# A two-layer decoder trunk on one core: expert tiles turned on another engine, gates placed a step later, scores a step later, one affine cut into pieces

## The chip, the cores and the metric

The kernel runs as one program on 1 core of one Trainium2 chip. The metric is the device time of that core in microseconds, the median of the runs shown. The core has five engines with in-order instruction queues of their own: TensorE (PE, with its weight loads shown as PEld), VectorE (DVE), ScalarE (ACT), GpSimd (POOL) and SyncE (SP, which here only issues DMAs).

## The reference

The computation is a decoder trunk with D = 1024, 256 tokens, batch 1 and 2 layers. Each layer does two things to the residual x:

```python
# part 1: two token mixers side by side
mod = silu(c) @ w_ada[l] + b_ada[l]                  # six rows: shift, scale, gate, twice
hm  = x * (1 + sc1) + sh1
qa, fa, ia, ga, qb, kb, vb, gate_a, gate_b = split(hm @ w_in[l])
oa  = rms_norm(hgrn2(qa, fa, ia)) * silu(ga)         # S_t = f_t S_{t-1} + (1-f_t) v_t, o_t = S_t' q_t
ob  = stick_breaking_attention(qb, kb, vb)
y   = (sigmoid(gate_a) * (oa @ w_up_a) + sigmoid(gate_b) * (ob @ w_up_b)) @ w_o
x   = layer_norm(ALPHA * x + y * gt1, ln_g[l, 0], ln_b[l, 0])
# part 2: product-key experts: 16384 experts of one neuron each, 8 heads, 16 chosen per head and token
hf  = x * (1 + sc2) + sh2
idx, gates = top16 of the sums of two top16 lists of 128 keys, softmax     # per token and head
y   = sum over the chosen experts of gate * gelu(hf . peer_u[idx]) * peer_v[idx]
x   = layer_norm(ALPHA * x + y * gt2, ln_g[l, 1], ln_b[l, 1])
```

## The kernel before

**Precision and matmuls.** Every float32 weight is split into a high part (`wh`, a rounded copy made by ACT) and a low part (`wl`, the rest, a subtraction made by POOL or DVE, line 271). A product is three matmuls: high by high, high by low, low by high (`products`, line 63). Nearly all of them go through `mm` at line 61, so the profile puts them on one line; what they write tells them apart: `A` is the expert scores, `Y` the expert output, `T`, `G` and `K` are further PSUM tiles.

**How weights arrive.** `order` (lines 101 to 177) is one list of all weight tiles of 128 x 1024 in the order of their use. `take` (line 302) hands the next one out: it first issues the DMA of a later tile (`fetch`, on SP's queue), then has the tile after the current one split (`prep`, line 227: ACT makes `wh`, POOL or DVE makes `wl`), and then has the next `u` tile turned (`turn`, line 215). All engines get their instructions in this written order; nothing is reordered later.

**The mixers** (`mixers`, line 656). The projections walk over weight tiles, 24 matmuls each. After each tile `project` calls `pull` (line 635), which lets a side generator issue some of its own work: first `decays`, then `hgrn`, then `stick`. `hgrn` (line 819) computes the intra-sequence scores of the recurrence as a tree of 9 levels (sizes 256, 128, ..., 2, 1). Level i goes through four stages: exponents (`st_exp`: two DVE subtractions, one ACT exponential), products (`st_mul`: two DVE multiplications into a tile named `qk`), scores (`st_score`: 8 or 4 small matmuls) and placing (`st_place`: two masked DVE copies). Step i of its loop (line 890) issues placing of level i-3, scores of level i-2, products of level i-1 and exponents of level i, and ends with `yield None`, which lets `pull` do no more than one step for each weight tile. `qk` has two buffers; `stick` and, at the start of the program, the loads of `w_ada` (`mtile`, line 1060) use the same tile name, and SP waits in order until a buffer is free.

**The experts** (`peer`, line 1319). Instead of gathering experts, all 16384 are computed densely. 128 `u` tiles give the scores (`u_tile`, line 1623: 24 matmuls of 128 x 128 by 128 x 256), 128 `v` tiles the output (line 1710 on: 12 matmuls of 512 columns). The gates are zero where an expert was not chosen. A `u` tile must be turned so that the model dimension lies on the partitions, and there are two ways for it. Kind "u" is loaded in rows of 1 KB and turned in 32 x 32 blocks by one DVE instruction (line 220). Kind "x" is loaded in pieces of 128 bytes, and is turned by 8 TensorE transposes (line 251), after which ACT copies each half out of PSUM twice (lines 263 and 264). `uv_seq` (line 124) makes every fourth tile an "x".

Beside the `u` tiles runs one side generator, `select`. First `topk` finds the 16 best of each head (many small DVE instructions, then for each half of the tokens the selection from line 1449, with six large DVE instructions of 128 x 2048). Then `place_gates` (line 1492) goes through 64 blocks of 4 tokens. For each block, `build` makes two one-hot tiles (DVE, lines 1499 and 1504), `prod` multiplies them into a PSUM tile `G` (8 small matmuls), and `put` writes the result to the activations: by ACT where the scores of an expert tile are not there yet, by a DVE multiplication (line 1531) where they are. Step b issues `prod` of block b-1, `build` of block b, then `put` of block b-1.

**The budget.** Each `u` tile calls `pull(sides, 1.55 + 1.2 * (kind == "x"))` (line 1642). Each `yield c` of a generator takes c from this credit, a negative credit ends the turn, and `yield None` ends it too. The numbers c are meant as microseconds of DVE, but they are only what is written there. After tile 125 whatever is left of the side work is issued at once (`drain`, line 1645).

**The affine of the first norm** is applied late: at `v` tiles 38 and 44 (line 1725), POOL multiplies one half of x by the row `g_row` and adds `b_row`, in whole instructions of 128 x 1024. Both rows come by a POOL-issued DMA (`load_row`) into space that `v` tiles 12 to 19 set free.

Of the kernel before, what the change touches and what calls it, by code (L numbers as in the profile page):

```python
# [16 lines left out]
P = 128  # L17
# [28 lines left out]
def trunk_kernel(ctx: ExitStack, tc: tile.TileContext, x, c, w_ada, b_ada, w_in, lb_logits, hg_norm_g,  # L46
# [76 lines left out]

    uv_seq = [("x" if j % 4 == 3 else "u", j) for j in range(NK)] + [("v", j) for j in range(NK)]
    for l in range(DEPTH):
# [530 lines left out]
    def mixers(l, hT):  # L656
        with ExitStack() as es:
# [161 lines left out]
            def hgrn():  # L819
# [28 lines left out]
                def st_mul(i):  # L848
                    n = sizes[i]
                    if n == 1:  # L850
                        return
                    hn = n // 2
                    t = ap.tile([P, HG_H, S], F32, name="qk", bufs=2)
                    ev = es_.pop(i)
                    tv = nodes(t, n)
                    nc.vector.tensor_mul(tv[:, :, :hn], nodes(kk, n)[:, :, :hn], ev[:, :, :hn])
                    nc.vector.tensor_mul(tv[:, :, hn:], nodes(qT, n)[:, :, hn:], ev[:, :, hn:])  # L857
                    qk[i] = t
# [30 lines left out]
                n = len(sizes)  # L889
                for i in range(n + 3):  # L890
                    if 0 <= i - 3 < n:
                        st_place(i - 3)
                    if 0 <= i - 2 < n:
                        st_score(i - 2)
                    if 0 <= i - 1 < n:
                        st_mul(i - 1)
                    yield 2.4
                    if i < n:
                        st_exp(i)
                    yield None  # L900
# [44 lines left out]
            def stick():  # L945
# [17 lines left out]
                def mask(z, a):  # L963
                    sp = ap.tile([P, HG_H, S], F32, name="qk", bufs=2).rearrange("p h t -> p (h t)")[:, :384]
                    nc.vector.scalar_tensor_tensor(sp, z[:, :384], 0.0, a, op0=OP.max, op1=OP.add)
# [79 lines left out]
            def start():  # L1045
# [14 lines left out]
                def mtile():  # L1060
                    names.rotate(1)
                    return ap.tile([P, HG_H, S], F32, name=names[0], bufs=2).rearrange("p h t -> p (h t)")

# [171 lines left out]
            else:  # L1235
# [16 lines left out]
                    (("f_z", 1), ("qT", 1), ("qbT", 1), ("kbT", 1), ("v_a", 1), ("v_b", 1), ("kk", 1), ("bb", 1),  # L1252
                     ("gaT", 1), ("sc0", 1), ("e", 2), ("e", 2), ("qk", 2), ("qk", 2))]
            free = deque(a[:, i] for a in free for i in range(2))
# [64 lines left out]
    def peer(l, hT):  # L1319
        with ExitStack() as es:  # L1320
# [11 lines left out]
            with ExitStack() as eu:  # L1332
# [26 lines left out]
                def topk():  # L1359
# [89 lines left out]
                    for tt in range(2):  # L1449

                        puf = pu[tt].rearrange("p h k -> p (h k)").bitcast(U32)
                        for a in range(2):
                            nc.vector.tensor_scalar(sel[a].bitcast(U32), puf, 4 - 2 * a, None,
                                                    op0=OP.logical_shift_right)
                            nc.vector.tensor_copy(half[2 + a], iu[a][tt].rearrange("p h k -> p (h k)").bitcast(U32))

                        nc.vector.scalar_tensor_tensor(half[0], sel[1].bitcast(U32), -12.0, sel[0].bitcast(U32),
                                                       op0=OP.add, op1=OP.max)
                        for a in range(2):
                            nc.vector.scalar_tensor_tensor(sel[a], half[0], -16.0 + 12 * a, puf, op0=OP.mult, op1=OP.add)  # L1460
                        nc.vector.scalar_tensor_tensor(half[1], sel[1], -48.0, sel[0], op0=OP.add, op1=OP.max)
                        tp = top[tt]
                        yield 0.9
                        for a in range(2):
                            nc.vector.tensor_tensor(m, per_head(half[a])[:, :, :, None].to_broadcast(k4),
                                                    iota_k[:, None, None].to_broadcast(k4), op=OP.is_equal)
                            yield 1.4
                            nc.vector.tensor_mul(m, m, per_head(half[2 + a])[:, :, None].to_broadcast(k4))
                            yield 1.1
                            nc.vector.tensor_reduce(per_head(sel[a]), m, axis=mybir.AxisListType.X, op=OP.add)  # L1470
                            yield 1.4
                        nc.vector.tensor_reduce(sm[:, :PH], tp, axis=mybir.AxisListType.X, op=OP.add)
# [19 lines left out]
                def place_gates():  # L1492
# [26 lines left out]
                    def put(b, pg):  # L1519
# [12 lines left out]
                        progress["t"] = (b + 1) * TB  # L1532

                    built, prods = {}, {}
                    nb = S // TB
                    for b in range(nb + 1):
                        if 0 <= b - 1 < nb:
                            prods[b - 1] = prod(b - 1)
                        if b < nb:
                            build(b)  # L1540
                        yield 1.2
                        if 0 <= b - 1 < nb:
                            put(b - 1, prods.pop(b - 1))

                        yield 0.2 + 0.7 * progress["j"] / NK
                        yield None
# [163 lines left out]
                for kind, j in uv_seq[nu:]:  # L1710
# [13 lines left out]

                    if j in (NB_J + 6, NB_J + 12):
                        xb = from_blocks(xt[j // 6 - (NB_J + 6) // 6])
                        nc.gpsimd.tensor_mul(xb, xb, in_blocks(g_row))
                        nc.gpsimd.tensor_add(xb, xb, in_blocks(b_row))
                    mod_step(mods_left)
# [55 lines left out]
```

## Time and profile before

| What | Value |
|---|---|
| median of 3 runs | 2251.29 us (2247.49 to 2252.64) |
| profiled execution | 2254.38 us, its span 2252.6 us, granted TensorE clock 0.982 |
| busy: PE, DVE, ACT, POOL | 2135.2, 1817.2, 1172.5, 1041.5 us |
| HBM read | 396.46 MB, 176 GB/s over the span |

The stages of layer 0 as the trace shows them: start to about 105 us, tree of scores to 160 us, other mixer work to 303 us, `u` tiles from about 309 to 777 us, `v` tiles to about 1135 us. Layer 1 repeats them from there (tree 1214 to 1262 us, `u` tiles to 1883 us, `v` tiles to 2230 us).

A row of the groups reads: line, engine, operation, what it writes and reads, shape, count, then busy time in us and the mean of one in ns, then idle time of the engine just before and what ended it. A row of a window reads: the stretch, its length, busy time (and count of instructions) of PE, PEld, DVE, ACT and POOL, then the granted clock, the DMA share and GB/s. A row of the timeline reads: start, length, engine, line, operation, count, and in brackets the idle time before it. A matmul's own duration is longer than the distance between two of them, since they overlap; so PE's costs are taken from busy time and from periods.

### The profile page before, as it was taken

To read this page: it belongs to the slowest core of one execution; us is meant where nothing else is said; L and a number is where in the kernel's file an instruction comes from. 1 tells how busy PE (TensorE), PEld (TensorE's weight loads), DVE (VectorE), ACT (ScalarE), POOL (GpSimd) and SP (SyncE) were. 2 spreads that over 40 slices of the span, in tenths; PEclk is the share of its full clock that TensorE was granted. 3 is DMA by queue.
4 is the path that set the end of the run, shared out by engine and by line. 5 is a ranking of instruction groups with operands and counts; after the bars stand their busy time and mean duration, and the time that the engine had idled before them with its cause. 6 is when DMAs were issued, how large, how long until landed. Compare 5 with 4: busy or idle time off the path is not lost.

```text
span 2252.6 us, 42211 instructions
## 1 busy us (share of the span) xinstructions
PE 2135.2 (95%) x14596; PEld 1945.4 (86%) x14596; DVE 1817.2 (81%) x3278; ACT 1172.5 (52%) x2445; POOL 1041.5 (46%) x760
## 2 busy tenths in 40 slices
PE   5789899899999999999989998998999999999998
PEld 5789799899999978888779897997999999788886
DVE  7887989999997488888887558999999955666675
ACT  3446555455555545555545564554555555455562
POOL 4656637787778510000045534577777783200001
PEclk8999999999999999999999999999999999999999
DMA  8646567666667678888844335675766676666662
GB/s 273 196 137 221 159 140 159 129 148 148 142 147 156 176 236 275 281 286 283 298 134 150 113 121 142 147 153 118 154 142 148 146 164 187 202 196 192 193 227 90
DMA packets 498895, 400.32 MB, mean 178 GB/s; under 512 B 291920, under 2 KB 446072, under 8 KB 498680
## 3 DMA queue, kind: packets, MB, share of 16 engines
q1 hardware_dynamic: 496936, 392.33, 62.8%
q0 software_dynamic: 1408, 4.23, 0.6%
q8 instruction: 115, 1.88, 0.3%
q10 hardware_dynamic: 336, 1.06, 0.1%
q14 instruction: 100, 0.82, 0.1%
HBM read 396.46 MB, written 1.05 MB: 176 GB/s over the span
## 4 chain that ended last, share of the span: by engine, by line
PE 73%; DVE 16%; DMA 4%; issue 3%; ACT 3%; POOL 1%; SPq 1%; POOLq 0%; ACTq 0%; DVEq 0%
PE A L61 28%; PE Y L61 27%; PE T L61 7%; PE G L61 4%; PE T L251 2%; DVE wl L271 2%; PE ss L61 2%; PE hs L61 2%; DMA raw<-in_peer_u_dram 2%; POOL wl L271 1%; DVE qk L857 1%; DMA raw<-in_peer_v_dram 1%; DVE raw L220 1%; DVE e L843 1%; DVE o L1504 1%
## 5 line engine op out<-in xcount | busy, mean ns | idle before, releaser
L271 POOL TENSOR_TENSOR wl<-raw,wh 128x512 fp32r<-128x512 f32 x663 | 914.3, 1406 | 700.9 <-ACT wh L58 582.4
L58 ACT ACTIVATE wh<-raw 128x512 fp32r<-128x512 f32 x1060 | 610.8, 623 | 182.0 <-PE A L61 47.6
L61 PE MATMUL A<-hTh,wh 128*128 128x256 f32 x2080 | 543.3, 293 | 11.9 <-ACT wh L58 11.8
L61 PE MATMUL A<-hTl,wh 128*128 128x256 f32 x2080 | 524.2, 284 | 0.0
L61 PE MATMUL Y<-wh,o 128*128 128x512 f32 x1776 | 480.5, 392 | 0.8 <-DVE o L521 0.8
L271 DVE TENSOR_TENSOR wl<-raw,wh 128x512 fp32r<-128x512 f32 x525 | 380.2, 765 | 63.5 <-ACT wh L58 44.9
L61 PEld LDWEIGHTS A<-hTh,wh 128*128 128x128 f32 x2080 | 400.6, 193 | 14.4 <-ACT wh L58 13.7
L61 PEld LDWEIGHTS A<-hTl,wh 128*128 128x128 f32 x2080 | 401.7, 193 | 0.8 <-DVE hTl L521 0.2
L61 PEld LDWEIGHTS Y<-wh,o 128*128 128x128 f32 x1776 | 334.9, 189 | 70.8 <-DVE o L521 1.2
L61 PE MATMUL A<-hTh,wl 128*128 128x256 f32 x2080 | 337.9, 285 | 11.0 <-POOL wl L271 10.9
L61 PEld LDWEIGHTS A<-hTh,wl 128*128 128x128 f32 x2080 | 288.9, 193 | 14.2 <-POOL wl L271 14.2
L61 PE MATMUL Y<-wl,o 128*128 128x512 f32 x888 | 277.9, 393 | 10.4 <-DVE wl L271 10.4
L220 DVE STREAM_TRANSPOSE raw<-raw 128x1024 f32<-128x1024 f32 x192 | 235.1, 1230 | 11.7 <-DMA raw<-in_peer_u_dram 10.1
L58 ACT ACTIVATE o<-buf 128x256 fp32r<-128x256 f32 x228 | 95.1, 417 | 282.7 <-PE Y L61 282.7
L521 DVE TENSOR_TENSOR o<-buf,o 128x256 fp32r<-128x256 f32 x228 | 100.1, 439 | 150.4 <-ACT o L58 150.4
L61 PEld LDWEIGHTS Y<-wl,o 128*128 128x128 f32 x888 | 168.1, 189 | 48.9 <-DVE wl L271 13.8
L1499 DVE TENSOR_TENSOR o<-iT,iota_t 128x1024 f16<-128x1024 f16 x128 | 163.9, 1280 | 0.0
L58 ACT ACTIVATE buf<-G 128x128 f32<-128x128 f32 (+4 forms) x244 | 56.0, 276 | 203.6 <-PE G L61 203.6
L570 POOL TENSOR_TENSOR x<-x,buf 128x1024 f32<-128x1024 f32 x1 | 2.4, 2392 | 291.0 <-DVE x L567 291.0
L61 PE MATMUL T<-hTh,wh 128*128 128x256 f32 x512 | 133.6, 293 | 0.0
L61 PE MATMUL T<-hTl,wh 128*128 128x256 f32 x512 | 130.1, 286 | 0.0
L1504 DVE TENSOR_TENSOR o<-gT,o 128x1024 f16<-128x1024 f16 x128 | 124.6, 973 | 4.4
(496 smaller groups left out, 3254.9 us busy)
## 6 DMA issues: line engine op xcount, KB each, us to landing
raw<-in_peer_u_dram SPq DMA_DIRECT2D x1024, 128.0 KB, 3.5
raw<-in_peer_v_dram SPq DMA_DIRECT2D x256, 512.0 KB, 4.4
raw<-in_w_in_dram SPq DMA_DIRECT2D x88, 512.0 KB, 4.9
raw<-in_w_ada_dram SPq DMA_DIRECT2D x78, 512.0 KB, 4.9
raw<-in_w_o_dram SPq DMA_DIRECT2D x16, 512.0 KB, 3.5
raw<-in_w_pq_dram SPq DMA_DIRECT2D x64, 128.0 KB, 3.4
qk<-in_w_ada_dram SPq DMA_DIRECT2D x10, 512.0 KB, 3.9
e<-in_w_ada_dram SPq DMA_DIRECT2D x8, 512.0 KB, 6.0
```

What stands on the lines that cost most here:

```text
L58: nc.scalar.activation(o, i, f, **kw)
L61: nc.tensor.matmul(o, a, b, start=start, stop=stop, **kw)
L220: nc.vector.transpose(t, t)
L251: nc.tensor.transpose(banks[s][:, q], t[:, (4 * s + q) * P:(4 * s + q + 1) * P], ident)
L271: eng.tensor_sub(lo, src, h.bitcast(F32))
L521: nc.vector.tensor_sub(lo, src, h.bitcast(F32))
L570: nc.gpsimd.tensor_mul(xt[tt], xt[tt], last[0])
L843: eng.tensor_sub(ev[:, :, :hn], mid, bv[:, :, :hn])
L857: nc.vector.tensor_mul(tv[:, :, hn:], nodes(qT, n)[:, :, hn:], ev[:, :, hn:])
L1499: nc.vector.tensor_tensor(o.rearrange("p a u n v -> p (a u) n v"), iT[:, b].rearrange("p a (u v) -> p (a u) v", v=2)[:, :, None] .to_broad ...
L1504: nc.vector.tensor_mul(og.rearrange("p u a n v -> p (u a) n v"), gT[:, b * nu:(b + 1) * nu].rearrange("p u a v -> p (u a) v")[:, :, None] ...
```

## The change

- **Tiles turned.** In the second half of the `u` tiles (j from 64 on) kind "x" becomes "u": 16 tiles in each layer lose their 8 TensorE transposes and two of four ACT copies, and get one DVE transpose and the loads in rows of 1 KB instead of 128 bytes. Their budget falls from 2.75 to 1.55.
- **Block order.** `place_gates` puts block b-2 first, then builds block b, then multiplies block b-1; so a `put` comes a step after its `prod`. There is one more step.
- **Budget of the selection.** More yields and larger numbers: 13.0 instead of 8.7 for each half of the tokens up to line 1471. The instructions stay the same.
- **Tree.** Scores of level i-3 and placing of level i-4 instead of i-2 and i-3, one more step, three `qk` buffers instead of two; with that the `w_ada` loads at the start get a third `qk` buffer too.
- **Affine in pieces.** 16 POOL instructions of 128 x 256 at `v` tiles 38 to 53, instead of 4 of 128 x 1024 at tiles 38 and 44.

```diff
-    uv_seq = [("x" if j % 4 == 3 else "u", j) for j in range(NK)] + [("v", j) for j in range(NK)]
+    uv_seq = [("x" if j % 4 == 3 and j < NK // 2 else "u", j) for j in range(NK)] + [("v", j) for j in range(NK)]
...
-                    t = ap.tile([P, HG_H, S], F32, name="qk", bufs=2)
+                    t = ap.tile([P, HG_H, S], F32, name="qk", bufs=3)
...
-                for i in range(n + 3):
+                for i in range(n + 4):
+                    if 0 <= i - 4 < n:
+                        st_place(i - 4)
                     if 0 <= i - 3 < n:
-                        st_place(i - 3)
-                    if 0 <= i - 2 < n:
-                        st_score(i - 2)
+                        st_score(i - 3)
                     if 0 <= i - 1 < n:
                         st_mul(i - 1)
                     yield 2.4
...
-                    return ap.tile([P, HG_H, S], F32, name=names[0], bufs=2).rearrange("p h t -> p (h t)")
+                    return ap.tile([P, HG_H, S], F32, name=names[0], bufs=3 if names[0] == "qk" else 2).rearrange("p h t -> p (h t)")
...
                         for a in range(2):
                             nc.vector.tensor_scalar(sel[a].bitcast(U32), puf, 4 - 2 * a, None,
                                                     op0=OP.logical_shift_right)
+                            yield 0.5
                             nc.vector.tensor_copy(half[2 + a], iu[a][tt].rearrange("p h k -> p (h k)").bitcast(U32))
+                            yield 0.6
 
                         nc.vector.scalar_tensor_tensor(half[0], sel[1].bitcast(U32), -12.0, sel[0].bitcast(U32),
                                                        op0=OP.add, op1=OP.max)
+                        yield 0.5
                         for a in range(2):
                             nc.vector.scalar_tensor_tensor(sel[a], half[0], -16.0 + 12 * a, puf, op0=OP.mult, op1=OP.add)
+                            yield 0.5
                         nc.vector.scalar_tensor_tensor(half[1], sel[1], -48.0, sel[0], op0=OP.add, op1=OP.max)
                         tp = top[tt]
-                        yield 0.9
+                        yield 0.5
                         for a in range(2):
                             nc.vector.tensor_tensor(m, per_head(half[a])[:, :, :, None].to_broadcast(k4),
                                                     iota_k[:, None, None].to_broadcast(k4), op=OP.is_equal)
-                            yield 1.4
+                            yield 1.7
                             nc.vector.tensor_mul(m, m, per_head(half[2 + a])[:, :, None].to_broadcast(k4))
                             yield 1.1
                             nc.vector.tensor_reduce(per_head(sel[a]), m, axis=mybir.AxisListType.X, op=OP.add)
-                            yield 1.4
+                            yield 1.6
...
-                    for b in range(nb + 1):
-                        if 0 <= b - 1 < nb:
-                            prods[b - 1] = prod(b - 1)
+                    for b in range(nb + 2):
+                        if b >= 2:
+                            put(b - 2, prods.pop(b - 2))
+
+                            yield 0.2 + 0.7 * progress["j"] / NK
                         if b < nb:
                             build(b)
-                        yield 1.2
-                        if 0 <= b - 1 < nb:
-                            put(b - 1, prods.pop(b - 1))
-
-                        yield 0.2 + 0.7 * progress["j"] / NK
+                            yield 1.2
+                        if 1 <= b <= nb:
+                            prods[b - 1] = prod(b - 1)
                         yield None
...
-                    if j in (NB_J + 6, NB_J + 12):
-                        xb = from_blocks(xt[j // 6 - (NB_J + 6) // 6])
-                        nc.gpsimd.tensor_mul(xb, xb, in_blocks(g_row))
-                        nc.gpsimd.tensor_add(xb, xb, in_blocks(b_row))
+
+                    n = j - NB_J - 6
+                    if 0 <= n < 16:
+                        xb = from_blocks(xt[n // 8])[:, n % 4]
+                        (nc.gpsimd.tensor_add if n // 4 % 2 else nc.gpsimd.tensor_mul)(
+                            xb, xb, in_blocks(b_row if n // 4 % 2 else g_row)[:, n % 4])
```

The other hunks give three buffers to the remaining uses of the tile name `qk`.

More of the change, by code (lines that the diff above doesn't have):

```diff
@@ L963, in mask @@
                 def mask(z, a):
-                    sp = ap.tile([P, HG_H, S], F32, name="qk", bufs=2).rearrange("p h t -> p (h t)")[:, :384]
+                    sp = ap.tile([P, HG_H, S], F32, name="qk", bufs=3).rearrange("p h t -> p (h t)")[:, :384]
                     nc.vector.scalar_tensor_tensor(sp, z[:, :384], 0.0, a, op0=OP.max, op1=OP.add)
@@ L1252, in mixers @@
                     (("f_z", 1), ("qT", 1), ("qbT", 1), ("kbT", 1), ("v_a", 1), ("v_b", 1), ("kk", 1), ("bb", 1),
-                     ("gaT", 1), ("sc0", 1), ("e", 2), ("e", 2), ("qk", 2), ("qk", 2))]
+                     ("gaT", 1), ("sc0", 1), ("e", 2), ("e", 2), ("qk", 3), ("qk", 3))]
             free = deque(a[:, i] for a in free for i in range(2))
```

## The prediction

> **What bounds the kernel now.** I read the page's busy times first, then TensorE's waits, then busy times by stage, then groups inside the stages.
>
> ```profile
> PE 2135.2 (95%) x14596; PEld 1945.4 (86%) x14596; DVE 1817.2 (81%) x3278; ACT 1172.5 (52%) x2445; POOL 1041.5 (46%) x760
> ...
> PE hs L61 <- DVE qk L857: 20.9, 14, 7.5
> PE A L61 <- ACT wh L58: 11.8, 7, 2.3
> PE A L61 <- POOL wl L271: 10.9, 15, 1.3
> ```
>
> PE is busy 95%, so 117 us of the span are left to gain from waits (2252.6 - 2135.2), and beyond that only PE work that is taken away counts. The change touches the waits shown, 20.9 us at the tree's scores and 22.7 us in the `u` tiles, and holes in the `v` tiles. Where they lie, by stage (PE busy is the second number behind the stretch, DVE the fourth):
>
> ```profile
> 416.00:471.00 55.00, 45.84 (x340) 43.80 (x341) 53.00 (x59) 24.32 (x45) 43.71 (x28) 0.94 0.58 125
> 548.00:706.00 158.00, 157.69 (x1472) 154.36 (x1470) 155.31 (x229) 87.55 (x232) 122.14 (x88) 1.00 0.65 146
> 706.00:777.00 71.00, 70.97 (x600) 70.76 (x599) 31.74 (x39) 38.89 (x73) 56.06 (x44) 1.00 0.72 167
> 826.00:846.00 20.00, 14.38 (x48) 10.73 (x47) 19.48 (x16) 5.82 (x12) 10.46 (x5) 0.84 0.63 207
> 860.00:1080.00 220.00, 220.00 (x988) 181.88 (x988) 180.87 (x298) 118.38 (x242) 0.00 (x0) 1.00 0.85 283
> ...
> 1508.00:1574.00 66.00, 54.62 (x408) 51.82 (x407) 64.58 (x103) 29.30 (x53) 45.34 (x31) 0.95 0.59 122
> 1931.00:1951.00 20.00, 15.26 (x57) 11.60 (x56) 15.75 (x15) 6.65 (x14) 11.59 (x7) 0.87 0.56 165
> ```
>
> The rows say: while gates are placed (548 to 706 us) PE and DVE are both full, 157.7 and 155.3 of 158 us. Only after that (706 to 777) does DVE have air: 39 us. In the selection (416 to 471) PE idles 9.2 us behind a full DVE, in layer 1 (1508 to 1574) 11.4 us. In the `v` tiles PE is full except for one hole in each layer, 5.6 and 4.7 us.
>
> **The `u` tiles: fewer transposes, more DVE.** Groups of 548 to 706 us, and two pieces of the chain after the gates:
>
> ```profile
> L1499 DVE TENSOR_TENSOR o<-iT,iota_t 128x1024 f16<-128x1024 f16 x43 | 52.1, 1212 | 0.0
> L220 DVE STREAM_TRANSPOSE raw<-raw 128x1024 f32<-128x1024 f32 x33 | 40.6, 1232 | 0.0
> L1504 DVE TENSOR_TENSOR o<-gT,o 128x1024 f16<-128x1024 f16 x42 | 38.9, 927 | 1.5
> L1531 DVE TENSOR_TENSOR buf<-G,buf 128x128 f32<-128x128 f32 (+4 forms) x89 | 23.4, 306 | 0.0
> L1618 DVE TENSOR_TENSOR buf<-A,buf 128x168 f32<-128x168 f32 (+21 forms) x22 | 10.7, 487 | 1.2 <-ACT A L58 1.1
> ...
> L61 PE MATMUL A<-hTh,wh 128*128 128x256 f32 x348 | 90.6, 293 | 0.0
> L61 PE MATMUL G<-o,o 128*128 128x128 f16 x341 | 27.1, 220 | 0.3
> L251 PE MATMUL T<-ident,raw 128*128 128x128 f32 x88 | 11.4, 273 | 0.0
> ...
> 709.29 11.51 PE A L61 x96
> 721.68 11.51 PE A L61 x96
> ```
>
> PE: four tiles take 11.51 us (2.88 a tile), and their period is 12.39, so one tile's 8 transposes cost 0.88. In the 158 us lie 348/8 = 43.5 tiles (3.63 a tile), 341/8 = 42.6 blocks and 88/8 = 11 turned tiles; a block costs PE (158 - 43.5 x 2.88 - 11 x 0.88)/42.6 = 0.54. DVE: the five groups sum to 165.7 us, but instructions overlap and busy time is 155.3, a factor 0.937. A transpose then costs 1.155, a block 2.52 (1.212 + 0.927 + 23.4/42.6, times 0.937), the multiplication of line 1618 0.23 a tile.
>
> The written budgets give how many blocks go with a tile. A block takes 1.2 + 0.2 + 0.7 x share of tiles done, about 1.8, and four tiles bring 3 x 1.55 + 2.75 = 7.4: one block a tile, as the counts above show. From tile 64 on a tile brings 1.55. Counting the credit through both versions, the first block moves from tile 40 to 44 (the selection's larger numbers), 20 instead of 24 blocks are built by tile 63, the rest come at 0.82 a tile, and the last is put at tile 118 instead of 105. So nothing is left for the drain after tile 125.
>
> Tiles 64 to 118, each: DVE 1.155 + 0.82 x 2.55 (the later blocks have a little more to multiply) + 0.23 = 3.48; PE 2.88 + 0.82 x 0.54 = 3.32. **DVE sets the pace**, and 54 tiles take 188 us, where now 42 take 3.63 and 12 take 3.10, 189.7 us: 1.8 us won, though PE loses 16 x 0.88 = 14 us of work. The last 10 tiles go from 3.10 to 2.88: 2.2 us. Before tile 64, four blocks fewer are 10.1 us less for a DVE that is full; PE could give up 9.2 us of idle and 4 x 0.54: I take 10. Together 14 in each layer; 1 off for two full engines that never mesh quite: **26 us** for both. Bounds: if PE set the pace throughout, 11.4 (13.6 in layer 1) + (189.7 - 54 x 3.32) + 2.2 = 24 and 26, so 50; below, the rivals.
>
> What depends on what: ACT loses 32 copies a layer, but is busy only 87.6 of 158 us; DMA is at 0.65 and gets longer rows; both count nothing, and SP issues four loads a tile either way. The block order takes ACT's wait for `prod` away:
>
> ```profile
> ACT buf L58 <- PE G L61: 203.6, 128, 2.9
> ```
>
> That is 1.6 us a block, behind which the next tile's `wh` stands. PE does not wait there now, so by itself it is worth nothing; it is the slack that lets DVE be late without PE noticing.
>
> A rule that bears on the DVE price: the Trainium skill, "SBUF — State Buffer", section "Who interferes with whom", says that a DVE instruction with two SBUF inputs and a GpSimd instruction that reads SBUF block each other for a whole instruction, and one with a single input doesn't. The trace agrees: the transpose (one input) is 1.23 us throughout, the two builds of a block swing:
>
> ```profile
> L1499 DVE TENSOR_TENSOR o<-iT,iota_t x43: 697/1249/1484, 547.9 to 705.3; 128x1024 f16<-128x1024 f16 x43
> L1504 DVE TENSOR_TENSOR o<-gT,o x42: 691/692/1715, 549.3 to 702.4; 128x1024 f16<-128x1024 f16 x42
> ```
>
> **The affine in pieces.** POOL's row and DVE's rows of the hole at 826 to 846 us:
>
> ```profile
> 837.15 2.58 POOL L1727 TENSOR_TENSOR x<-x,buf 128x1024 f32<-128x1024 f32 x1
> ...
> 827.98 3.85 DVE L271 TENSOR_TENSOR wl<-raw,wh 128x512 fp32r<-128x512 f32 x2
> 834.84 2.64 DVE L521 TENSOR_TENSOR o<-buf,o 128x256 fp32r<-128x256 f32 x1 [0.27 <-ACT o L58]
> 837.40 5.62 DVE L271 TENSOR_TENSOR wl<-raw,wh 128x512 fp32r<-128x512 f32 x2
> 842.94 0.41 DVE L521 TENSOR_TENSOR o<-buf,o 128x256 fp32r<-128x256 f32 x1
> 843.28 1.28 DVE L271 TENSOR_TENSOR wl<-raw,wh 128x512 fp32r<-128x512 f32 x2
> ```
>
> Undisturbed, these DVE instructions take 1.28 and 0.41; DVE is late by 2.57 + 2.23 + 4.34 = 9.1 us, and PE idles 5.6. The pieces don't spread over 16 tiles: POOL has nothing else to do here (0.00 busy from 860 on) and waits only for the two rows' loads, so all 16 run back to back, at 2.58/4 = 0.65 each. A DVE instruction then waits for 0.65 at most. DVE's idle time, 39 of 220 us, is 0.48 in each of the 988/12 = 82 tiles; twelve pieces alternating with DVE instructions of about 0.64 last 15.5 us, 5.8 tiles, and these absorb 2.8 of at most 7.8 us, beside the tile that is prepared ahead. I take two thirds of the holes: **6.5 us** of 10.3; bounds 0 (each piece makes one instruction wait in full: 16 x 0.65 = 10.4, no less than now) and 10.3.
>
> **The tree.**
>
> ```profile
> 109.66 1.13 ACT L58 ACTIVATE wh<-raw 128x512 fp32r<-128x512 f32 x2
> 112.31 2.05 PE L61 MATMUL hs<-qk 128*128 128x128 f32 x8 [7.48 <-DVE qk L857]
> ...
> 127.93 1.80 DVE L857 TENSOR_TENSOR qk<-qT,e 128x512 f32<-128x512 f32 x1
> 129.65 1.75 DVE L843 TENSOR_TENSOR e<-bb 128x512 f32<-128x512 f32 x1
> 132.10 1.06 ACT L58 ACTIVATE e<-e 128x1024 f32<-128x1024 f32 x1 [3.77 <-DVE e L844]
> 133.06 1.14 ACT L58 ACTIVATE wh<-raw 128x512 fp32r<-128x512 f32 x2
> 138.13 1.06 ACT L58 ACTIVATE e<-e 128x1024 f32<-128x1024 f32 x1 [3.44 <-DVE e L844]
> ```
>
> PE waits for the products of the level just made. But the loop that sets the pace has no PE in it: products, subtractions of the next level (DVE), exponential (ACT), products again; from one exponential to the next it takes 6.0 us (132.10 to 138.13). And ACT splits the next weight tile behind that exponential (133.06). With scores a step later PE finds them ready, does a tile instead, and then waits for the next `wh`. So of the 20.9 us I count only the ends: the first wait (until 112.31; a tile is ready from 109.66: 2.6 us, layer 0) and one score group of 2 us done before the loop ends instead of after, 1.5 a layer: 5.6 together. Against it stands one more step, which shifts `stick` by a weight tile, so that one or two of its steps run alone at the end; at 1.8 us a layer, 3.6. **Net 2 us**; bounds 20.9 won and 4 lost.
>
> **The start.** The third `qk` buffer lets two loads pass that now hold SP up ahead of a weight tile for which ACT waits:
>
> ```profile
> 24.64 0.39 SPq L199 DMA_DIRECT2D qk<-in_w_ada_dram  x1
> 26.39 1.01 SPq L199 DMA_DIRECT2D raw<-in_w_in_dram  x2
> 33.52 2.37 ACT L58 ACTIVATE wh<-raw 128x512 fp32r<-128x512 f32 x4 [13.00 <-DMA raw<-in_w_in_dram]
> ```
>
> The second of the two then goes at 24.64 and the weight tile 1.3 us earlier: **1 us**, bounds 0 and 3.
>
> **Sum.** 26 + 6.5 + 2 + 1 = 35.5 us off the profiled execution's 2254.4 (span 2252.6 and 1.8 around it) gives 2218.9. The median of the runs shown lies 3.1 lower than that execution, so I predict **2216 us** for the median.
>
> **Rivals and chances.** What a measurement of this kernel can tell from no change is about 0.2%, 4.5 us.
>
> - Forecast, 2200 to 2232: 0.50.
> - PE sets the pace (0.13, below 2200): DVE's builds collide less once ACT and POOL run ahead. Then 50 + 10 + 6 + 2 = 68 us, 2183. For it: L1504 takes 0.69 when nothing blocks it. Against: DVE's 155.3 of 158 now.
> - DVE takes the gain back (0.20, 2232 to 2247): each tenth of a us more in a tile costs 54 x 0.1 x 2 = 11 us. At 3.72 instead of 3.48 the `u` tiles win nothing, and 9.5 us remain: 2242.
> - No change (0.07): the same at 3.8.
> - Slower (0.10): DVE, now the engine waited for, always meets POOL's pair of subtractions for the same tile, and L1504 stands at its 1.715 each time: 0.79 x 0.937 x 0.82 = 0.61 more a tile, 66 us, 2282. It decides from 0.33 a tile on, a mean of 1.36 for L1504. Against it: now half of them take 0.69.
> - By the skill's rule each piece of the affine blocks anew, so cutting wins nothing: 6.5 us less in any of these cases (a quarter); the forecast would be 2222.
>
> Faster 0.50 + 0.13 + 0.20 = 0.83, same 0.07, slower 0.10. The range 2188 to 2250 leaves out about 0.05 below and 0.13 above.
>
> **What would show it.** PE transposes 256 instead of 512, DVE transposes 224. Gates of layer 0 placed until about 730 us, DVE full until then, and PE idle by a tenth or two of a us a tile: right; PE full as now: the second case. L1504's mean above 1.36: slower. No POOL instruction of the affine above 0.7 us and holes below 2 us: right. The tree's loop still at about 6 us a level. The prediction is wrong if the `u` tiles of a layer don't shrink by 8 to 20 us.

## The result, and the profile after

The changed kernel takes 2277.4 us (2275.1 to 2278.5) beside 2251.0 us for the kernel before (median of four runs): a ratio of 1.0118, interval [1.0101, 1.0136]. It is **1.2% slower**, where 2216 us were forecast. Its profiled execution took 2278.5 us.

The page after, busy times, and TensorE's waits:

```profile
PE 2118.5 (93%) x14340; PEld 1918.7 (84%) x14340; DVE 1887.8 (83%) x3323; ACT 1133.5 (50%) x2371; POOL 1097.2 (48%) x785
...
PE G L61 <- DVE o L1508: 42.7, 56, 2.0
PE A L61 <- ACT wh L58: 15.7, 12, 2.3
PE ss L61 <- DVE mh L1143: 15.6, 4, 5.3
PE A L61 <- POOL wl L271: 13.8, 26, 1.5
PE T L61 <- DVE wl L271: 11.7, 4, 4.9
PE T L61 <- ACT qbT L58: 8.5, 3, 6.2
PE hs L61 <- ACT sc L58: 5.6, 2, 2.9
```

PE lost 16.7 us of work (2135.2 to 2118.5), DVE gained 70.6, and a wait stands at the top that did not exist: PE's block products wait 42.7 us for DVE's second build (the old L1504 is now L1508, the old L1499 is L1503, L1531 is L1535, L1618 is L1623). The two builds over the whole run, with minimum, median and maximum in ns; before first, after second:

```profile
L1499 DVE TENSOR_TENSOR o<-iT,iota_t x128: 644/1324/1780, 470.6 to 1811.6; 128x1024 f16<-128x1024 f16 x128
...
L1504 DVE TENSOR_TENSOR o<-gT,o x128: 691/692/1779, 471.3 to 1812.3; 128x1024 f16<-128x1024 f16 x128
```

```profile
L1503 DVE TENSOR_TENSOR o<-iT,iota_t x128: 643/668/1789, 481.4 to 1881.1; 128x1024 f16<-128x1024 f16 x128
...
L1508 DVE TENSOR_TENSOR o<-gT,o x128: 691/1670/1794, 482.1 to 1881.8; 128x1024 f16<-128x1024 f16 x128
```

The typical first build got fast (1324 to 668) and the typical second one slow (692 to 1670); 120 of the 128 second builds are slow. By the page's groups the means went from 1.280 + 0.973 = 2.253 us a block to 0.870 + 1.614 = 2.484.

**Where in the kernel.** Counted from the first tile of layer 0's `u` part, tile 38 starts 6.9 us earlier than before, tile 64 3.9 earlier, tile 118 18.7 *later*. Tiles 64 to 118, forecast at 188 us, take 213.0; before they took 190.5. The busy times of that stretch (its length, then PE, PEld, DVE, ACT, POOL), and DVE's and POOL's groups in it (busy us, mean ns):

```profile
554.00:767.00 213.00, 187.62 (x1659) 177.94 (x1657) 205.68 (x277) 89.33 (x235) 166.74 (x109) 1.00 0.49 134
...
L1508 DVE TENSOR_TENSOR o<-gT,o 128x1024 f16<-128x1024 f16 x45 | 75.1, 1668 | 1.5
L220 DVE STREAM_TRANSPOSE raw<-raw 128x1024 f32<-128x1024 f32 x55 | 67.1, 1227 | 0.0
L1503 DVE TENSOR_TENSOR o<-iT,iota_t 128x1024 f16<-128x1024 f16 x45 | 38.2, 848 | 0.0
...
L271 POOL TENSOR_TENSOR wl<-raw,wh 128x512 fp32r<-128x512 f32 x109 | 168.9, 1574 | 46.3 <-ACT wh L58 41.1 <-PE A L61 5.2
```

PE idles 25.4 us here, and DVE is full but for 7.3. A pair of builds is 1.668 + 0.848 = 2.516 us. The reason is in the timeline, DVE's rows first and then ACT's and POOL's; a row is start, duration, engine and line, and the bracket is the idle time before it:

```profile
622.08 1.23 DVE L220 STREAM_TRANSPOSE raw<-raw 128x1024 f32<-128x1024 f32 x1
623.24 0.51 DVE L1535 TENSOR_TENSOR buf<-G,buf 128x128 f32<-128x128 f32 x2
623.68 0.67 DVE L1503 TENSOR_TENSOR o<-iT,iota_t 128x1024 f16<-128x1024 f16 x1
624.38 1.67 DVE L1508 TENSOR_TENSOR o<-gT,o 128x1024 f16<-128x1024 f16 x1
...
623.47 1.16 ACT L58 ACTIVATE wh<-raw 128x512 fp32r<-128x512 f32 x2 [3.36 <-POOL wl L271]
...
624.18 3.02 POOL L271 TENSOR_TENSOR wl<-raw,wh 128x512 fp32r<-128x512 f32 x2 [0.88 <-ACT wh L58]
```

The end of a transpose starts two chains. ACT splits the tile, and POOL's first subtraction begins 0.7 us after ACT did, at 624.18. DVE meanwhile does the multiplications of `put` (0.51) and the first build (0.67), and so comes to the second build at 624.38, when POOL has been reading for 0.2 us. The build takes 1.67 instead of 0.69. The trace shows what it waits for: of the 120 slow second builds 113 end 0.55 us after the end of the subtraction that was running when they started, however much of that was left. The new order, `put` ahead of `build`, places it there in nearly every block.

### The profile page after: what moved, and what is told of

Its sections match the earlier page's. It is cut to its first block, busy times and chain, and to the rows that moved or that the text cites. A ratio compares the mean times of both kernels' runs of the same rounds, so it can differ in the third digit from the quotient of the medians.

```text
span 2276.7 us, 41892 instructions
## 1 busy us (share of the span) xinstructions
PE 2118.5 (93%) x14340; PEld 1918.7 (84%) x14340; DVE 1887.8 (83%) x3323; ACT 1133.5 (50%) x2371; POOL 1097.2 (48%) x785
## 3 DMA queue, kind: packets, MB, share of 16 engines
q8 instruction: 113, 1.85, 0.3%
## 4 chain that ended last, share of the span: by engine, by line
PE 55%; DVE 17%; issue 9%; POOL 8%; DMA 6%; ACT 3%; SPq 2%; POOLq 0%; DVEq 0%; ACTq 0%
PE Y L61 27%; PE A L61 14%; POOL wl L271 7%; PE T L61 6%; DMA raw<-in_peer_u_dram 5%; DVE wl L271 2%; PE ss L61 2%; PE hs L61 2%; PE G L61 2%; DVE o L1508 2%; SPq L197 1%; DVE raw L220 1%; DVE mh L381 1%; PE T L251 1%; ACT wh L58 1%
## 5 line engine op out<-in xcount | busy, mean ns | idle before, releaser
L271 POOL TENSOR_TENSOR wl<-raw,wh 128x512 fp32r<-128x512 f32 x664 | 959.5, 1472 | 666.4 <-ACT wh L58 600.9
L58 ACT ACTIVATE wh<-raw 128x512 fp32r<-128x512 f32 x1124 | 647.3, 622 | 457.9 <-POOL wl L271 238.7
L220 DVE STREAM_TRANSPOSE raw<-raw 128x1024 f32<-128x1024 f32 x224 | 273.6, 1228 | 0.8 <-DMA raw<-in_peer_u_dram 0.5
L1508 DVE TENSOR_TENSOR o<-gT,o 128x1024 f16<-128x1024 f16 x128 | 206.6, 1614 | 4.4
L61 PE MATMUL G<-o,o 128*128 128x128 f16 x1024 | 81.1, 220 | 42.7 <-DVE o L1508 42.7
L1503 DVE TENSOR_TENSOR o<-iT,iota_t 128x1024 f16<-128x1024 f16 x128 | 111.4, 870 | 0.0
```

What stands on the lines that cost most here:

```text
L58: nc.scalar.activation(o, i, f, **kw)
L61: nc.tensor.matmul(o, a, b, start=start, stop=stop, **kw)
L220: nc.vector.transpose(t, t)
L271: eng.tensor_sub(lo, src, h.bitcast(F32))
L1503: nc.vector.tensor_tensor(o.rearrange("p a u n v -> p (a u) n v"), iT[:, b].rearrange("p a (u v) -> p (a u) v", v=2)[:, :, None] .to_broad ...
L1508: nc.vector.tensor_mul(og.rearrange("p u a n v -> p (u a) n v"), gT[:, b * nu:(b + 1) * nu].rearrange("p u a v -> p (u a) v")[:, :, None] ...
```

## The experiments

Two theories stood against the **order theory** just told. In the transpose theory 16 more transposes overfill DVE whatever the order; in the budget theory 0.82 block a tile, alternating full and empty tiles, is the harm.

**1. The tiles alone.** On the kernel before:

```
-    uv_seq = [("x" if j % 4 == 3 else "u", j) ...
+    uv_seq = [("x" if j % 4 == 3 and j < NK // 2 else "u", j) ...
```

> The kernel before with one edit: the tiles of the second half of the `u` part are all turned by DVE. Block order, selection, affine and tree stay as before. Order theory (the new block order starts the second build of a block just when POOL has begun its subtraction, and that alone makes the DVE overrun): the second build keeps a mean of 0.9 to 1.1 us as before, tiles 64 to 118 take 188 to 195 us, the time is 2240 to 2252. Transpose theory (DVE is overfilled by 16 more transposes whatever the order): the second build rises to 1.4 us or more here too, tiles 64 to 118 take 205 us or more, the time is 2270 to 2300. Budget theory (0.82 block a tile makes full and empty tiles alternate): the second build stays near 1.0, but tiles 64 to 118 still take 200 or more, 2262 to 2275.

2254.1 us, ratio 1.0007 [0.9997, 1.0017]: no change, and 2 us above what the order theory expected. Tiles 64 to 118 take 193.7 us. DVE's groups there:

```profile
L1504 DVE TENSOR_TENSOR o<-gT,o 128x1024 f16<-128x1024 f16 x41 | 51.7, 1262 | 1.4
L1499 DVE TENSOR_TENSOR o<-iT,iota_t 128x1024 f16<-128x1024 f16 x41 | 38.3, 935 | 0.0
```

The transposes do move the meeting onto the second build (0.956 in the like stretch of before, 1.262 here, more than the order theory's 1.1), but the pair is 2.20, where it was 2.16. They give nothing, and they cost nothing like 26 us: the transpose and budget theories fall as the main cause.

**2. The order alone.** On the kernel before, only the loop of `place_gates` as in the change (`put(b - 2)`, `build(b)`, `prod(b - 1)`).

> The kernel before with one edit: the new block order (put two blocks back, build, product) and nothing else. Order theory: the second build rises from 0.97 to 1.4 us or more; DVE was at 155.3 of 158 us, so the `u` tiles get 5 to 20 us longer a layer: 2260 to 2290. Transpose theory: TensorE still sets the pace with the old mix of tiles, 2246 to 2256, whatever the second build takes. Budget theory: 2246 to 2256.

2290.2 us, ratio 1.0166 [1.0149, 1.0182], 37 us slower, at the upper end of what the order theory expected. The builds' means are 0.962 and 1.441, and in the stretch that was full before, neither engine is full:

```profile
557.00:700.00 143.00, 133.23 (x1216) 129.08 (x1215) 135.90 (x190) 70.32 (x193) 108.50 (x73) 0.99 0.55 133
```

PE idles 9.8 of 143 us. ACT, which must split each tile, waits as well, for engines that are themselves behind. PE's and ACT's waits in the same stretch:

```profile
PE G L61 <- DVE o L1504: 9.7, 12, 2.0
...
ACT wh L58 <- POOL wl L271: 44.0, 19, 3.3
ACT wh L58 <- PE T L251: 20.1, 6, 4.9
```

A tile turned by TensorE has its transposes in PE's queue behind the block's product; when that waits for a build, ACT, POOL and the next tile wait too. That chain is how I read a loss of 37 us where DVE's pairs grew by only 128 x 0.15 = 19; the next runs bear on what starts it.

**3. The order without POOL's reads.** On the kernel before and on the one with the new order, for the `u` part's tiles:

```
-            eng.tensor_sub(lo, src, h.bitcast(F32))
+            if kind in "ux" and eng is nc.gpsimd:
+                for _ in range(2):
+                    nc.gpsimd.memset(ls[s].bitcast(F32), 0.0)
+            else:
+                eng.tensor_sub(lo, src, h.bitcast(F32))
```

> The kernel before, with POOL's subtractions of the `u` part (tiles turned by DVE and by TensorE) replaced by fills with zero, two for each: the low part of these weights is left out of the result. It is the partner of order_writes: what the two differ by is what the block order costs without the port. TensorE set the pace after tile 40 already, so the gain is mostly the selection's, 14 us a layer by tile 64 in the run with fills on the kernel after: 2215 to 2230.

> The kernel before with the new block order alone, and POOL's subtractions of the `u` part replaced by fills with zero, two for each: the low part of these weights is left out of the result. If the order costs its 38 us through the port alone, this comes within 6 us of before_writes, both builds at 0.69. If the order also costs by its own chain (TensorE waits for a block's build, the next tile's transposes stand behind the product, ACT behind those), it is 12 us or more above before_writes, with TensorE waiting for the builds.

2216.56 and 2216.54 us, one run each. Within each layer the `u` tiles of the two start within 0.5 us of each other. Both builds run at 0.67 to 0.69 on average, and PE is full (161.0 of 161 us). So **the whole 37 us of the order go when POOL's subtractions go**; the chain through PE's transposes only carries them on. The fills also shorten POOL's work, so these two runs don't tell its reads from its time; experiment 9 keeps the subtractions and does.

The fills show something else that I had overlooked. They take 36 us off the kernel before in its old order too, and most of it before the first block is built: tile 38 starts 14.4 us earlier in layer 0 and 17.3 in layer 1. So in the kernel before POOL's subtractions cost more up to the end of the selection than in the blocks. The selection's multiplications of 128x2048 values take 1.21 us on average with the fills instead of 1.93; how much of the whole is such meetings and how much POOL's shorter work, no run separates.

**4. The same on the changed kernel** (`kind == "u"` in the condition above).

> The kernel after with POOL's two subtractions of a `u` tile turned by DVE replaced by two fills with zero of the same size, which read nothing: the low part of these weights is left out of the result. TensorE does the same multiplications. Port theory (a DVE instruction with two inputs from SBUF can't run beside a POOL instruction that reads SBUF): the second build takes 0.69 to 0.9 us in nearly all of its 128 runs, tiles 64 to 118 go below 195 us, the time is 2225 to 2245. If any POOL work beside it slows the second build (writes too): it stays above 1.3, 2260 to 2280.

2183.2 us in one run, 94 less than the changed kernel and far below what I expected. The second build over the run, and busy times around tiles 64 to 118 (178.9 us by their starts):

```profile
L1512 DVE TENSOR_TENSOR o<-gT,o x128: 691/692/695, 467.9 to 1784.1; 128x1024 f16<-128x1024 f16 x128
...
538.00:718.00 180.00, 180.00 (x1671) 178.02 (x1670) 159.14 (x280) 100.07 (x239) 114.65 (x220) 1.00 0.59 163
```

POOL's fills run beside 120 of these 128 builds, and none is stretched: 691 to 695 ns. PE is full, at 178.9/54 = 3.31 us a tile.

**5. `put` behind the builds.** On the changed kernel (lines joined here):

```
-                        if b >= 2: put(b - 2, ...); yield ...
                         if b < nb: build(b); yield 1.2
+                        if b >= 2: put(b - 2, ...); yield ...
```

> The kernel after with one move: the multiplications of a block follow the two builds of the next block instead of standing ahead of them, so that the second build starts some 0.5 us earlier against POOL's subtraction. Order theory: the mean of the second build falls from 1.61 to 1.2 or below, tiles 64 to 118 go from 213 to 190 to 200 us, the time is 2230 to 2255. Transpose theory: the two builds together still take 2.4 us or more, only which of the two is long changes, and the time is 2268 to 2282. Budget theory: 2260 to 2275.

2251.2 us, ratio to before 0.9999 [0.9989, 1.0010]: moving a piece of 0.5 us wins 26 us back. Tiles 64 to 118 take 200.2 us instead of 213.0 in layer 0 and 199.9 instead of 212.8 in layer 1, which is nearly all of it. The second build's mean is 1.29, not the 1.2 or below that the order theory expected. The rows show both cases side by side:

```profile
639.53 1.23 DVE L220 STREAM_TRANSPOSE raw<-raw 128x1024 f32<-128x1024 f32 x1
640.68 0.64 DVE L1503 TENSOR_TENSOR o<-iT,iota_t 128x1024 f16<-128x1024 f16 x1
641.36 0.69 DVE L1508 TENSOR_TENSOR o<-gT,o 128x1024 f16<-128x1024 f16 x1
...
643.62 0.45 DVE L1623 TENSOR_TENSOR buf<-A,buf 128x312 f32<-128x312 f32 x1
643.99 1.03 DVE L1503 TENSOR_TENSOR o<-iT,iota_t 128x1024 f16<-128x1024 f16 x1
645.05 1.67 DVE L1508 TENSOR_TENSOR o<-gT,o 128x1024 f16<-128x1024 f16 x1
```

Directly behind the transpose a pair takes 1.33; with the 0.45 us of L1623 between, it takes 2.70. So it is throughout tiles 64 to 118 of layer 0, from the first build's start to the second one's end: 1.37 in 18 of the 21 pairs directly behind a transpose, 2.4 to 3.3 in all 24 that have L1623 between.

**6. That multiplication behind the builds too**, without the tree's edit (the multiplication of a tile's result is issued after the side work instead of before it):

> The kernel after without the tree's edit, with a block's two builds as the first thing after a tile's transpose: ahead of the multiplications of a block (as put_behind) and ahead of the multiplication of the tile's own result too. Port theory: the builds are over when POOL's subtraction starts, the second build goes to 1.1 or below (1.28 in put_behind), the pair of builds below 2.1, and the time is 2222 to 2240. If it only moves the meeting from the one build to the other (pair still 2.2): 2240 to 2250.

2256.6 us, ratio 1.0018 [1.0008, 1.0028]: a miss for the order of issue as a remedy. In its tiles 64 to 118 the pair is 1.058 + 1.267, no better than in 5 (0.954 + 1.276), and a new wait came:

```profile
PE A L61 <- DVE buf L1622: 12.2, 9, 1.9
```

The later multiplication holds the PSUM bank of the next tile, and a DVE that is late once meets the subtraction of the tile before; so I read the rows, without a run of its own.

**7. The rest of the change.** The changed kernel with the old tiles, then each other part alone on the kernel before (selection's budgets; affine; tree), each exactly as in the change. The changed kernel with nothing but the old order put back was not run.

> The kernel after with the old mix of tiles: every fourth `u` tile is turned by TensorE in the second half too. All other parts of the change stay. Order theory: the second build still stands at 1.4 us or more, so DVE is overfilled here too and the `u` tiles win nothing over the kernel before; 2240 to 2260. Transpose theory: the whole loss goes, the selection's 4 to 7 us a layer and the affine's 4 to 6 a layer show, less some 3 for the tree: 2225 to 2238. Budget theory: as the transpose theory.

> The kernel before with one edit: the selection is cut into more and larger budgets (0.5 and 0.6 behind its small steps, 1.7 and 1.6 behind its large ones). Block order, tiles, affine and tree stay as before. Kept theory: TensorE idles less in the selection, 7 us are won by tile 38, 4 to 7 still at tile 64, and since TensorE sets the pace of the remaining tiles with the old order the blocks that come later fit: 4 to 7 us a layer stay, 2238 to 2244. Given-back theory: the four blocks that move behind tile 64 cost as much there as they saved (4 x 2.3 us of DVE): 2249 to 2254. Order of the start and of the tree unchanged.

> The kernel before with one edit: the affine on POOL in sixteen pieces, one at a tile, instead of two whole passes at two tiles. If the smaller holes of the `v` tiles in the changed kernel (4.4 and 5.8 us shorter a layer) come from the pieces: 2240 to 2244. If they came from the later end of the gates, which leaves the `v` tiles a different start: 2250 to 2253.

> The kernel before with one edit: the scores of the tree a step later, with three product tiles. By the trace of the changed kernel (first tile of the `u` part 2.3 us later, layer 1's mixers 1.2 us longer): 2254 to 2257. By the prediction's term (3 us won): 2247 to 2250. If the later start came from the selection's budgets instead: 2250 to 2253.

All but the tiles: 2270.9, ratio 1.0084 [1.0067, 1.0101], above the 2240 to 2260 that the order theory expected; even with the old mix of tiles the order more than eats what the others win. The budgets: 2243.1, 0.9965 [0.9952, 0.9978], a gain that lasts to the end. The affine: 2246.2, 0.9976 [0.9966, 0.9986], between the two forecasts. The tree: 2254.7, 1.0013 [1.0003, 1.0022], a small loss. By ratios the five parts alone give, in us, order +37.4, budgets -7.9, affine -5.4, tree +2.9, tiles +1.6: together +28.6, measured +26.6. That the sums agree is partly luck: all parts but the tiles add up to +27.0 and measure +18.9, so on top of the others the tiles cost 7.7 us and not 1.6.

The budgets and the affine together:

> The kernel before with the selection's new budgets and the affine in pieces, and nothing else. If the two gains are independent: 0.9965 x 0.9976 = 0.9941 of before, 2236 to 2240. If both draw on the same slack: 2241 to 2245.

2234.8 us, 0.9918 [0.9902, 0.9935]: faster than both kernels, and 18.5 us won where the two alone add up to 13.3.

**8. A larger budget** on the changed kernel (`pull(sides, 1.85 ...)` instead of 1.55 from tile 64 on):

> The kernel after with one number: a `u` tile of the second half pulls 1.85 instead of 1.55 of side work, so that one block goes with each tile instead of 0.82. Budget theory (full and empty tiles alternate, and that costs): 2255 to 2268. Port theory: each block still costs DVE a pair of 2.5 us, and the blocks only come earlier: 2270 to 2282.

2284.0 in one run, against 2277.4: not better, so the uneven budget isn't the harm. It is 2 us above the port theory's range; a pair of builds still takes 2.44 us over the run (2.484 in the changed kernel).

**9. All the work kept, one input of the builds out of SBUF.** The row of numbers and the gates are copied once a layer into one PSUM buffer, as 32-bit words, and the builds read them there (shortened):

```
+    pp = psk.tile([P, 1024], F16, name="pp", bufs=1)     # buffer K: 2 -> 1
+    nc.vector.tensor_copy(pp[:, :2 * NK].bitcast(U32), iota_t....bitcast(U32))
+    nc.vector.tensor_copy(pp[:, 512:].bitcast(U32), gT....bitcast(U32))
...
-    build: is_equal(iT, iota_t); mul(gT, o)
+    build: is_equal(iT, iota_p); mul(gP, o)
```

> The kernel after with all its work, but with the second input of the two builds of a block (the row of numbers for the first, the gates for the second) held in PSUM instead of SBUF; one PSUM buffer of the selection's is given up for it. If it takes two inputs from SBUF on DVE's side to meet POOL: neither build is ever stretched, each takes one fixed time, TensorE no longer waits for them. What that fixed time is no trace shows: if it stays at 0.69, 2190 to 2215; if PSUM halves the rate (about 1.2 each, a pair of 2.4 against 2.48), 2262 to 2280. If one input from SBUF is enough to meet POOL: the builds still swing up to 1.7 and the time is 2270 or more.

> The kernel before with the selection's new budgets, the affine in pieces and, in addition, the second input of the two builds held in PSUM. Against the same without PSUM (2234.8): with builds of a fixed 0.69, 2205 to 2225; with 1.2 each, 2230 to 2240 (TensorE sets the pace there, so a pair of 2.4 in place of 2.25 costs little); if one SBUF input still meets POOL, 2235 to 2245.

> As psum_inputs, and the tiles of the second half of the `u` part are all turned by DVE (16 fewer turned by TensorE a layer), in the old block order. With builds of 0.69 TensorE sets the pace and the tiles from 64 to 118 take 179 us as in the run with fills: 2180 to 2200. With 1.2 each DVE sets it: 3.5 us a tile, 2232 to 2245.

On the changed kernel, order and all: 2210.2 us, 0.9822 [0.9799, 0.9845]. The two builds over this run, busy times around tiles 64 to 118, and POOL's group there:

```profile
L1513 DVE TENSOR_TENSOR o<-pp,o x128: 690/691/693, 483.3 to 1812.0; 128x1024 f16<-128x1024 f16 x128
...
L1508 DVE TENSOR_TENSOR o<-iT,pp x128: 668/676/687, 482.6 to 1811.3; 128x1024 f16<-128x1024 f16 x128
...
552.00:732.00 180.00, 180.00 (x1671) 178.06 (x1670) 158.28 (x278) 100.37 (x240) 141.52 (x110) 1.00 0.55 162
...
L271 POOL TENSOR_TENSOR wl<-raw,wh 128x512 fp32r<-128x512 f32 x110 | 142.2, 1296 | 38.7 <-ACT wh L58 36.7 <-ACT buf L58 0.3
```

POOL reads two inputs from SBUF as before, DVE one, and no build is stretched any more, though POOL subtracts beside 126 of the 128 second builds; POOL's subtraction too falls, from 1.574 in the changed kernel to 1.296. PE is full. The old order with the new tiles, budgets and affine gives the same 2210.1 us, 0.9826 [0.9804, 0.9849], and in each layer the `u` tiles of the two kernels start within 1.5 us of each other: without the meeting the order costs and wins next to nothing (the two differ by the tree's edit too). It was expected at 2180 to 2200.

With the old tiles it is 2237.7, 0.9944 [0.9926, 0.9963]: no gain over 2234.8, and a miss, since 2205 to 2225 was expected for builds of 0.69. The `u` tiles up to 118 do win, 2.7 us in layer 0 and 3.7 in layer 1; the meeting cost little there, since PE set the pace. What is lost again is the price of the PSUM buffer given up. From PE's first work into buffer K to the first `u` tile it takes 11.7 to 13.3 us a layer in the four kernels of experiments 9 and 10, and 8.7 in all the others; PE has a wait there that the kernel of 2234.8 us did not have:

```profile
PE K L1600 <- DVE buf L1604: 3.3, 2, 1.6
```

**10. Five more tiles.** As the kernel of 2210.1 us, with the tiles from 44 on turned by DVE (`j < 44`).

> As psum_u, with five more tiles a layer (those from 44 on) turned by DVE instead of TensorE. With the builds' inputs in PSUM, TensorE is full from tile 44 to 64 and DVE is busy 52 of 71 us there. If TensorE sets the pace: 5 tiles x 0.88 us x 2 layers = 9 us less than psum_u, 2199 to 2204. If DVE's transposes, one to a tile and on time for ACT's split, set it: 2206 to 2212.

2201.9 us, 0.9779 [0.9761, 0.9796], 8.2 us less, where 5 x 0.88 x 2 = 8.8 were due. It is **2.2% faster than the kernel before**, the fastest of the kernels that leave no work out.

## Why the prediction was wrong, point by point

- **The block order, "by itself it is worth nothing". This step failed.** Alone it costs 37 us. I saw it as a question of who waits for whom, and ACT's wait that it removes as slack; but it also sets *when*, after a transpose, the second build starts, and so against which POOL instruction. I costed DVE's builds as durations to be kept, though the rows I quoted (697 to 1484, 691 to 1715) said that their length hangs on the moment.
- **The rival "slower" had the mechanism** (L1504 meeting POOL's pair, mean above 1.36; it is 1.61), its time of 2282 was near 2277, and it had a chance of 0.10. That its time came so near is partly luck. What I held against it, "now half of them take 0.69", took the meeting for chance; the order makes it a rule. Its price was put together wrongly: the first build gets shorter as the second gets longer, so the pair grew by 0.38 us in that stretch, about 0.38 x 0.94 x 45 = 16 us a layer instead of 33. The remainder of the 25 us above the forecast is DVE's own idle time (7.3) and slightly more and longer blocks.
- **Tiles 64 to 118, "DVE sets the pace" at 3.48.** It did, at 213.0/54 = 3.94. Without the meeting PE sets it at 3.31 (experiments 4 and 9); my price for that case was 3.32. PE's 0.88 us for a turned tile holds too (experiment 10).
- **Before tile 64, 10 us a layer.** 3.9 and 6.8 in the changed kernel; the budgets alone give 4.8 and 7.7 by tile 64 and keep 3.1 and 4.9 to tile 126. Half the size, right in kind.
- **The last tiles, 2.2 us.** From tile 118 to 126, eight of those ten, 23.1 instead of 24.8 us: 1.7, right.
- **The affine, 6.5 us; bounds 0 and 10.3.** 5.4 us alone: right. The price of a piece was not: twelve took

```profile
854.61 12.86 POOL L1734 TENSOR_TENSOR x<-x,buf 128x256 f32<-128x256 f32 x12 [3.55 <-DMA buf<-in_ln_b_dram]
...
840.00:860.00 20.00, 17.40 (x71) 13.86 (x69) 16.50 (x21) 8.71 (x18) 8.70 (x11) 0.91 0.84 295
860.00:880.00 20.00, 18.95 (x85) 14.80 (x84) 19.14 (x28) 8.90 (x19) 7.47 (x7) 1.00 0.73 244
```

  1.07 us each instead of 0.65, and holes of 2.6 + 1.1 us remain of 5.6. The case in which cutting wins nothing did not come.
- **The tree, 2 us won; bounds 20.9 won and 4 lost.** About 3 lost. The wait for the products (20.9) is gone from the list, but in the tree alone two others stand in it that before did not have:

```profile
PE T L61 <- ACT qbT L58: 8.4, 2, 6.5
PE hs L61 <- ACT sc L58: 5.5, 2, 2.9
```

  The loop without PE in it set the pace, as I wrote: from one exponential to the next it takes 5.8 to 6.1 us before and after. So the step at the end seems to cost more than the ends gave; no run tests that.
- **The start, 1 us.** Not to be told: in the kernels here the first `u` tile starts between 321.3 and 326.7 us with the third buffer, and between 321.3 and 328.3 without it.
- **The skill's rule.** The Trainium skill, "SBUF — State Buffer", section "Who interferes with whom", says that a DVE instruction with two SBUF inputs and a GpSimd instruction that reads SBUF exclude each other for a whole instruction, that a GpSimd instruction that only writes does not, and that the order of issue decides who blocks. The runs agree in all three: slow builds that end 0.55 us after POOL's subtraction does, and 0.69 with one input in PSUM; 691 to 695 ns beside fills; and 1.33 or 2.70 us a pair by 0.45 us of issue time. I cited it for the unit price and did not carry it into the edit that moved the issue.

## What to carry to other kernels

When a change moves an instruction whose duration swings between two values in the trace, ask what starts the other engine's instruction and where the moved one will stand against it; a swing is not a mean to be multiplied. Where two engines meet by construction, it is better to take one operand out of the memory they share than to tune the order: moving `put` won back 26 us here, moving the operand 67, though the PSUM buffer given up for it cost 3 to 4.6 us a layer. And the parts of a change are best timed alone, and then together, since they need not add up: two of these five won, and one undid them.

## What the runs showed of the hardware that was not expected

- A DVE multiplication or comparison of 128x1024 16-bit values takes 691 and 676 ns with one input in PSUM, nearly the same as undisturbed with both in SBUF (691 and 643). The Trainium skill, "VectorE: DVE Perf Modes", section "The perf-mode tier table", gives an instruction with two tensors and any PSUM operand the single rate in its table, half that of 16-bit values in SBUF; below the table it keeps the single rate for 32-bit values and lets others with a PSUM operand reach the double one. The measurement decides, and goes with the words below the table: the rate did not halve here.
- The new order made a loss of 37 us (128 pairs longer by 0.15 us are only 19) in a stretch where afterwards no engine was full. Experiments 3 and 9 show that it begins with POOL's reads; how it grows on the way, through ACT's 44.0 and 20.1 us of waits, is read from the trace and was not tested by itself.
